# One add of two output-projection weights moved from VectorE to an accumulating transfer, with all jobs in a new order

## The chip, the cores and the metric

The kernel runs on one core of one Trainium2 chip. The metric is the device time of one execution in microseconds (us), lower is better. The core has TensorE (PE), which multiplies matrices; VectorE (DVE) and ScalarE (ACT), which work elementwise; GpSimd (POOL), which here only issues transfers that add to their destination; and SyncE (SP), which issues plain transfers. Each of these takes its own instructions strictly in order, and they meet at semaphores.

## The reference

One layer of a decoder on 512 tokens of width 1024, in f32. Cut to what matters here:

```python
def _mixer(x, mem, ..., w_in, w_a_out, ..., w_b_out, w_kv, w_att_out, w_o):
    h = _rmsnorm(x, norm_mix_g)
    proj = h @ w_in                       # 11264 columns: gated conv, GLU, queries, three gates
    ...                                   # y_a: short conv; y_b: 31-tap conv; y_c: attention on 256 tokens
    g = jax.nn.sigmoid((p_g + b_gate).reshape(bsz, seq, N_BRANCH, D_MODEL))
    merged = g[:, :, 0] * y_a + g[:, :, 1] * y_b + g[:, :, 2] * y_c
    return merged @ w_o                   # w_o: 1024 x 1024

x = x + _mixer(x, ...)
x = x + _conv_ffn(x, ...)                 # up-projection, 3-tap conv, SiLU gate, down-projection
return _rmsnorm(x, norm_final_g)
```

## The kernel before

**Products.** Every f32 operand is split into two float32r parts: ACT casts it to its high part (`whi` for weights, line L1220), and DVE subtracts that from the operand to get the low part (`wlo`, L1224). A product is then three matmuls: high by high, high by low, low by high (L1171 to L1173, and L1424 for the large projections). The large projections, the output projection and the down-projection use a seven-product block scheme (Strassen's): of four weight blocks and four activation blocks, sums and differences are formed, and seven products take the place of eight. A group of such products is a *quad*, its products are numbered 1 to 7, and each needs its own weight sum, split into its own pair `whi`, `wlo`.

**Weight sums.** A block of weights comes from HBM by a plain transfer that SP issues (L1250), 512 KB each. A further block is added in place by a transfer with `accum_op=ALU.add` that POOL issues (L1374, L2479, L2486), which reads its source, adds it to the tile and writes the tile. For one product after the next the same tile goes through several such additions; each waits until the pair of the product before has been split off. There are 48 pairs of transfers for the input projection alone.

**The output projection** (`w_o`, stage "wo", at about 530 to 573 us) has products a, b, f, c, d, e, g, each in two halves i = 0, 1. For half i a tile x holds one weight block plus another (job `("wadd", "x", i)`, a POOL transfer), and a tile y holds a third block. d is split from y, with its low part made by ACT (`("wn", ...)`, a negated copy) and a POOL transfer (`("wl", ("wo", "d", i))`). Then `("wsum", i)` puts y + x into y: by DVE, L1640, 128x1024. c is split from that sum (`("wh", ("wo", "c", i))` on ACT, `("wl", ("wo", "c", i))` on DVE), and after it `("wadd", "y", i)` adds a last block for g.

**Convolution taps.** The 31-tap convolution runs beside the projections: ACT makes products of a tap (`tp`, L2137), pairs of them are joined by a POOL transfer from SBUF to SBUF (`("tj", p, s)`, L2143), and DVE adds them to an accumulator (L2149).

**Attention** takes its scores (job `("s", h, tp)`, L1171 to L1173 on `k` and `qh`, `ql`) from the scaled queries: ACT makes `qh` (L1940), DVE `ql` (L1944).

**The order.** Nothing is scheduled at run time. The table `PLAN` lists all 2457 jobs in the order in which their instructions are emitted, so each engine's queue is the table's subsequence for that engine. An entry holds the job's key, the buffer places that it takes (`wf3` is load buffer 3, `sb7` a slot on the right of SBUF, `ps0` a PSUM bank), and, for some transfers, a third item: the job whose last instruction the transfer must wait for, a *hold*, with which loads are paced. Where a job takes a place, it waits for all users of the tile that held the place before. `Jobs.run` goes through the table and checks that each job stands behind what it needs:

```python
        for key, given, *held in PLAN:
            engine, fn, after, take, use = self.jobs[key]
            ...
            fn()
            if len(code) > n_code:
                for other in held:
                    wait_for(self.tc, code[n_code], last[other])
```

There are 362 jobs on PE, 863 on DVE, 790 on ACT, 185 on POOL and 221 on SP.

Of the kernel before, what the change touches and what calls it, by code (L numbers as in the profile page):

```python
# [11 lines left out]
ALU = mybir.AluOpType  # L12
# [69 lines left out]
    (("mem tile", 0), "sb2"), (("ldm", 0, 0), ""), (("raw tile", "K"), "wf3"),  # L82
# [958 lines left out]
def hybrid_block_kernel(  # L1041
# [19 lines left out]
    nc = tc.nc  # L1061
    x, out = x[0], out[0]
# [2186 lines left out]
```

## Time and profile before

| | us |
|---|---|
| median of 3 runs | 890.8 |
| lowest and highest of them | 887.27, 891.45 |
| the profiled execution | 888.78 |
| its span on the core | 886.8 |
| PE busy | 878.7 |
| DVE busy | 827.2 |
| ACT busy | 701.4 |

The span is the time from the core's first to its last instruction; the profiled execution's own time is 2.0 us longer, for what lies around the span. The page gives the busy time of each engine, the chain of work that ended last, and the groups of instructions; the trace behind it answers for single stretches. On PE matmuls overlap: a row of a matmul shows its whole passage, and the next one starts before it ends, so the distance from start to start is what a matmul costs. PE's granted clock is full in all of the 40 slices of the page.

### The profile page before, as it was taken

What the parts mean: (1) busy time and instruction counts of PE and PEld (TensorE: products, weight loads), DVE (VectorE), ACT (ScalarE), POOL (GpSimd) and SP (SyncE); (2) the same over time, 40 slices, a digit from 0 to 9 for tenths busy, and PEclk for the clock granted to TensorE, in tenths of its full rate; (3) what the DMA queues carried; (4) which work ended last, traced back from release to release, by engine and by line L of the source; (5) the groups of instructions that cost most, each with busy time, mean ns of one, the idle gap of its engine ahead of it and who ended that gap; (6) DMA issues with size and microseconds to landing.
All of it is one profiled execution on the core that took longest, in us unless ns stands there. A gap on an engine that the chain in (4) does not pass through costs nothing.

```text
span 886.8 us, 17492 instructions
## 1 busy us (share of the span) xinstructions
PE 878.7 (99%) x6937; PEld 848.8 (96%) x6937; DVE 827.2 (93%) x949; ACT 701.4 (79%) x983; POOL 168.3 (19%) x193
## 2 busy tenths in 40 slices
PE   9999999999999999999999999999999999999997
PEld 8999999999999999999899998899999999998886
DVE  6997889989999999999899999998899799999997
ACT  7587889979998788798889973877776677866665
POOL 0012222111222131221221211121121111101120
PEclk9999999999999999999999999999999999999999
DMA  9989999779999999998999999999999799689984
GB/s 352 340 194 234 228 254 233 143 148 211 248 232 265 235 266 218 240 245 223 245 228 257 238 251 283 300 261 244 240 236 260 177 262 190 160 284 331 268 180 131
DMA packets 62288, 211.38 MB, mean 238 GB/s; under 512 B 6784, under 2 KB 11776, under 8 KB 62208
## 3 DMA queue, kind: packets, MB, share of 16 engines
q0 software_dynamic: 28944, 96.00, 59.1%
q1 hardware_dynamic: 32976, 114.02, 35.6%
q8 instruction: 54, 0.88, 0.4%
q10 hardware_dynamic: 288, 0.27, 0.1%
q14 instruction: 26, 0.21, 0.1%
HBM read 194.23 MB, written 4.19 MB: 224 GB/s over the span
## 4 chain that ended last, share of the span: by engine, by line
PE 85%; DVE 6%; DMA 3%; ACT 3%; issue 2%; SPq 0%; POOL 0%; DVEq 0%; ACTq 0%
PE bank L1424 61%; PE bank L1173 6%; PE bank L1171 6%; PE bank L1172 6%; PE bank L1810 2%; DVE wlo L1224 2%; PE bank L2331 1%; PE bank L2333 1%; PE bank L2332 1%; DMA wf<-in_w_in 1%; DMA tp<-tp 1%; ACT whi L1220 1%; DVE fl L1338 1%; DMA wf<-in_w_v 1%; ACT tp L2137 1%
## 5 line engine op out<-in xcount | busy, mean ns | idle before, releaser
L1224 DVE TENSOR_TENSOR wlo<-wf,whi 128x1024 fp32r<-128x1024 f32 (+1 forms) x189 | 226.0, 1209 | 13.5 <-ACT whi L1220 13.1
L1220 ACT CAST whi<-wf 128x1024 fp32r<-128x1024 f32 x192 | 198.1, 1042 | 42.6 <-PE bank L1424 13.0
L2137 ACT ACTIVATE tp<-u,pk 128x495 f32<-128x495 f32 (+22 forms) x184 | 119.2, 712 | 4.7 <-DVE acc L2149 1.9
L2149 DVE TENSOR_TENSOR acc<-acc,tp 128x966 f32<-128x966 f32 (+17 forms) x74 | 87.7, 1185 | 4.0 <-DMA tp<-tp 2.1
L1374 POOL DMA_DIRECT2D wf<-in_w_in x48 | 45.9, 990 | 137.1 <-DVE wlo L1224 63.3
L1424 PE MATMUL bank<-fb10h,whi 128*128 128x256 f32 x232 | 64.1, 276 | 0.3 <-ACT bank L1458 0.3
L1424 PE MATMUL bank<-ft4h,whi 128*128 128x256 f32 x232 | 64.0, 276 | 0.0
L1424 PE MATMUL bank<-fb11h,wlo 128*128 128x256 f32 x232 | 63.9, 275 | 0.0
L1424 PE MATMUL bank<-ft7h,whi 128*128 128x256 f32 x232 | 63.9, 275 | 0.0
L1424 PE MATMUL bank<-fb11h,whi 128*128 128x256 f32 x232 | 63.9, 275 | 0.0
L1424 PE MATMUL bank<-fb00h,whi 128*128 128x256 f32 x232 | 63.9, 275 | 0.0
L1424 PE MATMUL bank<-fb00l,whi 128*128 128x256 f32 x232 | 63.8, 275 | 0.0
L1424 PE MATMUL bank<-fb00h,wlo 128*128 128x256 f32 x232 | 63.8, 275 | 0.0
L1424 PE MATMUL bank<-fb10l,whi 128*128 128x256 f32 x232 | 63.8, 275 | 0.0
L1424 PE MATMUL bank<-fb10h,wlo 128*128 128x256 f32 x232 | 63.8, 275 | 0.0
L1424 PE MATMUL bank<-ft5l,whi 128*128 128x256 f32 x232 | 63.8, 275 | 0.0
L1424 PE MATMUL bank<-ft5h,wlo 128*128 128x256 f32 x232 | 63.8, 275 | 0.0
L1424 PE MATMUL bank<-ft6l,whi 128*128 128x256 f32 x232 | 63.8, 275 | 0.0
L1424 PE MATMUL bank<-ft6h,wlo 128*128 128x256 f32 x232 | 63.8, 275 | 0.0
L1424 PE MATMUL bank<-ft7l,whi 128*128 128x256 f32 x232 | 63.8, 275 | 0.0
L1424 PE MATMUL bank<-ft7h,wlo 128*128 128x256 f32 x232 | 63.8, 275 | 0.0
L1424 PE MATMUL bank<-ft4l,whi 128*128 128x256 f32 x232 | 63.8, 275 | 0.0
(434 smaller groups left out, 3371.3 us busy)
## 6 DMA issues: line engine op xcount, KB each, us to landing
wf<-in_w_in POOLq DMA_DIRECT2D x48, 512.0 KB, 7.9
wf<-in_w_in SPq DMA_DIRECT2D x45, 512.0 KB, 6.4
wf<-in_w_up SPq DMA_DIRECT2D x29, 512.0 KB, 6.2
wf<-in_w_up POOLq DMA_DIRECT2D x26, 512.0 KB, 8.2
wf<-in_w_down SPq DMA_DIRECT2D x15, 512.0 KB, 5.3
wf<-in_w_a_out SPq DMA_DIRECT2D x8, 512.0 KB, 5.6
wf<-in_w_v SPq DMA_DIRECT2D x7, 512.0 KB, 6.1
wf<-in_w_kv SPq DMA_DIRECT2D x7, 512.0 KB, 6.8
```

Source lines behind the costliest of these rows:

```text
L1171: nc.tensor.matmul(ps, s_hi, w_hi, start=start, stop=False, skip_group_check=again)
L1172: nc.tensor.matmul(ps, s_hi, w_lo, start=False, stop=False, skip_group_check=again)
L1173: nc.tensor.matmul(ps, s_lo, w_hi, start=False, stop=stop, skip_group_check=again)
L1220: nc.scalar.copy(parts[0], src())
L1224: nc.vector.tensor_tensor(lo, src(), hi.bitcast(F32), op=ALU.subtract)
L1338: nc.vector.tensor_tensor(t, x, y.bitcast(F32), op=ALU.subtract)
L1374: nc.gpsimd.dma_start(out=tiles[key], in_=block(w, col[c], k), accum_op=ALU.add)
L1424: nc.tensor.matmul(ps[:, c, :], w[:, i, at], in_turns(a[i]), start=first and n == 0, stop=i == 3 and n == 2, skip_group_check=again,)
L1810: nc.tensor.matmul(ps[:, j, :], w[:, k, at], in_turns(a[:, k, :]), start=first and j == 0 and k == 0 and n == 0, stop=g == 1 and k == 3 an ...
L2137: nc.scalar.activation(two(("tp", p, s))[:, j, s:], two(("u", p))[:, j, : SEQ - s], AF.Copy, scale=weight(j),)
L2149: nc.vector.tensor_tensor(a, a, two(("tp", p, at))[:, :, at:], op=ALU.add)
L2331: nc.tensor.matmul(ps, w_hi[:, i, at], hi, start=first, stop=False)
```

## The change

`("wsum", 0)` becomes a POOL transfer that adds tile x to tile y inside SBUF; `("wsum", 1)` stays on DVE. The job needs what it needed before, and c's first half is split from its result as before.

```diff
         deferred.append(lambda i=i: job(
             ("wsum", i), "DVE", dve(1024), lambda: add_into(("wo", "y", i), ("wo", "x", i)),
-            [("wadd", "x", i), ("wl", ("wo", "d", i))], use=[("wo", "x", i), ("wo", "y", i)]))
+            [("wadd", "x", i), ("wl", ("wo", "d", i))], use=[("wo", "x", i), ("wo", "y", i)])
+            if i else job(
+            ("wsum", i), "POOL", MORE, lambda: nc.gpsimd.dma_start(
+                out=tiles["wo", "y", i], in_=tiles["wo", "x", i], accum_op=ALU.add),
+            [("wadd", "x", i), ("wl", ("wo", "d", i))], MORE_LATENCY,
+            use=[("wo", "x", i), ("wo", "y", i)]))
```

The whole table `PLAN` is replaced: the same jobs in another order, with other buffer places and other holds. Of PE's 362 jobs 89 change their rank, by at most 6 places; of DVE's 653, of ACT's 612, of POOL's 99 and of SP's 157, by up to 34. Two of its lines:

```diff
-    (("ld", ("raw", ("K", 0, 1))), "wf0", ("mh", 0, 0)), (("V", 0, 0), ""),
...
+    (("V0",), "ps0 ps2"), (("mh", 0, 1), ""), (("wl0", "V"), ""), (("ldm", 1, 0), "", ("warm",)),
```

What moved is shown at three places. The first is POOL's queue at the output projection (`whol` is a low part that a transfer finishes, `wo` the tiles x and y and that of e). Before:

```order
L1241 DMA whol_824_6423<-in_w_o 128x1024
L2479 DMA wo_847_6612<-in_w_o 128x1024
L1241 DMA whol_861_6718<-in_w_o 128x1024
L2479 DMA wo_855_6678<-in_w_o 128x1024
L1241 DMA whol_879_6855<-in_w_o 128x1024
L2479 DMA wo_876_6847<-in_w_o 128x1024
L2479 DMA wo_884_6878<-in_w_o 128x1024
L2486 DMA wo_854_6649<-in_w_o 128x1024
L2486 DMA wo_869_6807<-in_w_o 128x1024
```

and after:

```order
L1240 DMA whol_810_6315<-in_w_o 128x1024
L2478 DMA wo_820_6392<-in_w_o 128x1024
L2478 DMA wo_852_6648<-in_w_o 128x1024
L1240 DMA whol_862_6720<-in_w_o 128x1024
L2485 DMA wo_856_6681<-wo_820_6392 128x1024
L1240 DMA whol_881_6859<-in_w_o 128x1024
L2478 DMA wo_877_6851<-in_w_o 128x1024
L2478 DMA wo_884_6877<-in_w_o 128x1024
L2490 DMA wo_856_6681<-in_w_o 128x1024
L2490 DMA wo_870_6806<-in_w_o 128x1024
```

The new transfer (L2485) stands behind the one that finishes d's low part, and the addition into x's first half has moved up two places; behind the new one stand five more transfers of this stage. On DVE the add is gone there, and on PE the first group of d's matmuls, six of them, now stands ahead of c's first.

The second place is at about 183 to 191 us, ahead of the scores of heads 2 and 3. DVE (`acc<-acc,tp` adds a tap, `ql` is the queries' low part), before:

```order
L1224 TENSOR_TENSOR wlo_315_2332<-wf_266_1956,whi_314_2331 128x1024
L2149 TENSOR_TENSOR acc_290_2143<-acc_290_2143,tp_300_2245 128x2x511
L2149 TENSOR_TENSOR acc_290_2143<-acc_290_2143,tp_307_2303 128x2x509
L1944 SCALAR_TENSOR_TENSOR ql_330_2405<-qq_288_2136,qh_323_2379 128x1024
L1944 SCALAR_TENSOR_TENSOR ql_332_2434<-qq_269_1963,qh_322_2377 128x1024
```

and after:

```order
L1223 TENSOR_TENSOR wlo_316_2353<-wf_280_2063,whi_315_2352 128x1024
L2148 TENSOR_TENSOR acc_295_2172<-acc_295_2172,tp_298_2211 128x2x511
L1943 SCALAR_TENSOR_TENSOR ql_324_2381<-qq_270_1991,qh_318_2359 128x1024
L1943 SCALAR_TENSOR_TENSOR ql_326_2392<-qq_271_1995,qh_323_2379 128x1024
L1223 TENSOR_TENSOR wlo_321_2369<-wf_299_2215,whi_320_2368 128x1024
```

The second tap's add has left the place ahead of the queries, and head 2's queries, which come first on PE, are now first here too (`qh_322` and `qh_318` are head 2's). Two things do not show in these rows. Head 2's `qh` took the place of a tile `tp` that a joining transfer read, and now takes one that attention's softmax has left. And on PE the 24 matmuls of product 5 of the quad `("gate", 2, 1)` stood ahead of these scores, and now stand behind them.

The third place is ACT at about 357 to 362 us (L1458 seeds one PSUM bank with another; `wf_521` before and `wf_557` after are the tile of weight sums of the quad `("bb", 1)`). Before:

```order
L1220 CAST whi_600_4661<-wf_583_4518 128x1024
L1220 CAST whi_602_4665<-('cv', 3)_524_3994 128x1024
L1220 CAST whi_604_4694<-wf_521_3988 128x1024
L1458 COPY bank_606_4698<-bank_599_4635 128x512
L2137 ACTIVATE tp_607_4701<-u_185_1225,pk_86 128x489 x2
```

and after:

```order
L1219 CAST whi_599_4659<-wf_527_4002 128x1024
L2136 ACTIVATE tp_601_4664<-u_178_1159,pk_86 128x489 x2
L1219 CAST whi_602_4669<-('bb', 1)_583_4494 128x1024
L1457 COPY bank_604_4696<-bank_598_4633 128x512
L1465 ACTIVATE B_606_4701<-bank_591_4564 128x2x256
L1219 CAST whi_607_4703<-wf_557_4280 128x1024
```

The copy of the bank stood behind the cast of the quad's weight sum, and now stands ahead of it.

## Rows read from the trace of the kernel before

**Rows 1.** Page, part 1: busy us, share of the span, instructions.

```profile
PE 878.7 (99%) x6937; PEld 848.8 (96%) x6937; DVE 827.2 (93%) x949; ACT 701.4 (79%) x983; POOL 168.3 (19%) x193
```

**Rows 2.** Chain that ended last: start us, us, what.

```profile
175.71 10.53 DMA tp<-tp
...
348.82 11.48 DMA wf<-in_w_in
...
582.96 190.28 PE bank L1424 x1704
```

**Rows 3.** Page, part 5: line, engine, operation, tiles, count; busy us, mean ns; idle before.

```profile
L1224 DVE TENSOR_TENSOR wlo<-wf,whi 128x1024 fp32r<-128x1024 f32 (+1 forms) x189 | 226.0, 1209 | 13.5 <-ACT whi L1220 13.1
L1220 ACT CAST whi<-wf 128x1024 fp32r<-128x1024 f32 x192 | 198.1, 1042 | 42.6 <-PE bank L1424 13.0
...
L1424 PE MATMUL bank<-ft5h,wlo 128*128 128x256 f32 x232 | 63.8, 275 | 0.0
```

**Rows 4.** Waits of PE: waited for; us in total, times, longest.

```profile
PE bank L1171 <- ACT ob L2032: 0.7, 1, 0.7
PE bank L1424 <- ACT bank L1458: 0.3, 1, 0.3
PE bank L1173 <- DVE ql L1944: 0.2, 1, 0.2
PE bank L1810 <- DVE wlo L1224: 0.2, 1, 0.2
PE bank L1173 <- DVE mgl L2527: 0.2, 1, 0.2
```

**Rows 5.** ACT in order of time, 186 us: start, us, what, idle before.

```profile
186.26 2.01 ACT L1940 ACTIVATE qh<-qq 128x1024 fp32r<-128x1024 f32 x2 [3.14 <-DMA tp<-tp]
```

**Rows 6.** DVE in order of time, at 186 and at 541 us.

```profile
186.26 2.48 DVE L2149 TENSOR_TENSOR acc<-acc,tp 128x1022 f32<-128x1022 f32 x2 [2.11 <-DMA tp<-tp]
188.65 2.35 DVE L1944 SCALAR_TENSOR_TENSOR ql<-qq,qh 128x1024 fp32r<-128x1024 f32 x2
...
540.93 1.21 DVE L1640 TENSOR_TENSOR wo<-wo,wo 128x1024 f32<-128x1024 f32 x1
542.06 1.81 DVE L2527 TENSOR_TENSOR mgl<-mg,mgh 128x512 fp32r<-128x512 f32 x2
```

**Rows 7.** POOL in order of time: the addition into x's first half.

```profile
532.04 0.86 POOL L2479 DMA_DIRECT2D wo<-in_w_o  x1 [1.26 <-PE bank L1424]
```

**Rows 8.** Line L2143, the joins inside SBUF: 18 transfers of about 500 KB.

```profile
DMA to landing us min/median/max: 4.9/7.0/10.5
```

**Rows 9.** Tile wo, 520 to 565 us: its transfers from HBM.

```profile
DMA to landing us min/median/max: 5.2/6.9/11.1
```

**Rows 10.** PE in order of time, at 550, 714 and 736 us.

```profile
550.24 0.38 PE L1171 MATMUL bank<-whi,mgh 128*128 128x512 f32 x1
550.46 0.38 PE L1172 MATMUL bank<-wlo,mgh 128*128 128x512 f32 x1
...
714.23 0.28 PE L1424 MATMUL bank<-ft6l,whi 128*128 128x256 f32 x1
...
735.78 0.28 PE L1424 MATMUL bank<-ft5h,wlo 128*128 128x256 f32 x1
```

**Rows 11.** Page, part 3: queue of POOL's transfers; packets, MB, share of 16 engines.

```profile
q0 software_dynamic: 28944, 96.00, 59.1%
```

**Rows 12.** Busy time by stretch: us, engines, clock, DMA share, GB/s.

```profile
480.00:545.00 65.00, 64.83 (x499) 61.93 (x498) 62.98 (x83) 53.14 (x71) 12.30 (x15) 1.00 1.02 260
545.00:600.00 55.00, 54.94 (x381) 51.13 (x380) 52.83 (x61) 40.48 (x56) 11.04 (x13) 1.00 1.03 269
```

**Rows 13.** Line L1250, the plain loads of weights that SP issues.

```profile
DMA to landing us min/median/max: 3.6/6.3/12.1
```

**Rows 14.** Line L1374, the additions into weight tiles that POOL issues.

```profile
DMA to landing us min/median/max: 5.5/8.0/12.5
```

More of the change, by code (lines that the diff above doesn't have):

```diff
@@ L534 @@
-    (("wl", (("gate", 1, 0), 7)), ""), (("tap", 3, 30), ""), ((("gate", 1, 1), 5), "ps6"),
-    (("wh", (("gate", 1, 1), 1)), ""), (("weigh", 0, 2, 1), ""),
[4 rows of a table removed]
-    (("mu", "low"), ""), (("weigh", 0, 2, 0), ""),
-    (("ld", ("raw", ("merge", 0, 3, 0))), "wf3", ("tap", 3, 27)), (("mu", "mean"), "ps0"),
-    (("wh", (("gate", 1, 0), 3)), ""), (("r7", ("gate", 1, 0)), ""), ((("gate", 1, 1), 1), "ps1"),
-    (("centre", 1), ""), (("wh", (("gate", 1, 1), 2)), ""), (("sum", 0, 2), "", ("mu", "mean")),
@@ L614 @@
-    (("sum", 1, 1, 0), ""), ((("out", 1, 1), 3), ""), (("r3", ("out", 1, 0)), ""),
-    (("mgh", "a", 1), ""), (("wl", ("wo", "a", 1)), ""), (("mgh", "b", 0), "sb3"),
-    (("wl", ("wo", "d", 0)), "", (("out", 1, 0), 3)), (("by3", ("out", 1, 0)), ""),
-    ((("out", 1, 1), 4), ""), (("mgl", "a", 1), ""), (("r3", ("out", 1, 1)), ""),
-    (("sum", 1, 0, 1), "sb12"), (("wadd", "x", 0), "", (("out", 1, 1), 3)),
[105 rows of a table removed]
-    ((("cf", 1, 1), "done"), ""), ((("cf", 1, 0), "done"), ""), (("silu", 1), ""),
[18 rows of a table removed]
-    ((("cf", 2, 1), "done"), ""), ((("cf", 2, 0), "done"), ""), (("silu", 2), ""),
[34 rows of a table removed]
@@ new lines @@
+    (("o", 3, 0), "ps6"), (("ptl", 2, 1), ""), (("wl", (("cv", 0), 1)), ""),
+    (("wh", (("gate", 2, 1), 7)), ""), (("s3", ("gate", 2, 1)), ""), ((("gate", 2, 1), 6), ""),
[26 rows of a table added]
+    (("wl", (("out", 2, 0), 2)), ""), (("tap", 1, 16), ""), ((("out", 2, 1), 1), "ps7"),
[4 rows of a table added]
+    (("wl", (("out", 2, 1), 5)), ""), (("wh", (("out", 2, 1), 2)), ""), (("tap", 1, 18), ""),
+    ((("out", 2, 0), 5), "ps1"), (("r1", ("out", 2, 1)), "ps4"), (("s6", ("out", 2, 1)), ""),
+    (("wl", (("out", 2, 1), 2)), ""), (("sigmoid", 2, 3), ""), (("by2", ("out", 2, 0)), ""),
@@ new lines @@
+    (("fl", "o2", "t6"), ""), ((("out", 2, 1), 2), ""), (("wh", (("out", 2, 0), 7)), ""),
+    (("s7", ("out", 2, 1)), "", (("out", 2, 1), 1)),
+    (("ld", (("out", 2, 0), "r")), "wf2", ("fl", "o2", "t6")), (("tp", 1, 21), "sb15"),
+    (("wl", (("out", 2, 0), 7)), ""), (("wh", (("out", 2, 0), 6)), ""), (("tap", 1, 19), ""),
[8 rows of a table added]
+    (("wh", (("out", 2, 0), 4)), ""), (("tap", 1, 22), ""),
[119 rows of a table added]
+    (("wh", (("gate", 0, 0), 2)), ""), (("tap", 2, 24), ""),
[21 rows of a table added]
+    (("tap", 2, 29), ""), (("s6", ("gate", 0, 1)), "", (("gate", 0, 1), 5)),
@@ new lines @@
+    ((("gate", 0, 1), 1), "ps2"), (("wh", (("gate", 0, 0), 3)), ""), (("tap", 3, 3), ""),
+    (("tp", 2, 30), "sb15"), (("r7", ("gate", 0, 0)), ""), (("tap", 3, 4), ""),
+    (("s7", ("gate", 0, 1)), "", ("wh", (("gate", 0, 1), 2))), ((("gate", 0, 0), 4), ""),
[3 rows of a table added]
+    (("tap", 2, 30), ""), (("wh", (("gate", 1, 0), 5)), ""),
+    (("ld", ("raw", ("merge", 0, 0, 0))), "wf0"), (("tp", 3, 7), "sb3"),
+    (("wl", (("gate", 0, 1), 6)), ""), ((("gate", 0, 0), 3), ""),
[6 rows of a table added]
+    (("r6", ("gate", 0, 1)), ""), (("wh", (("gate", 1, 0), 1)), ""), (("tap", 3, 8), ""),
@@ new lines @@
+    (("wh", ("merge", 0, 0, 1)), ""), (("tap", 3, 13), ""),
+    (("ld", ("raw", ("merge", 0, 2, 0))), "wf0", ("wl", ("merge", 0, 0, 0))), (("tap", 3, 14), ""),
+    (("tp", 3, 15), "sb7"), (("merge", 0, 0, 0), "ps2 ps0"), (("tp", 3, 18), "sb2"),
+    (("tap", 3, 15), ""), (("wl", ("merge", 0, 0, 1)), ""), (("tp", 3, 17), "sb7"),
+    (("tap", 3, 16), ""), (("ld", ("raw", ("merge", 0, 2, 1))), "wf3", (("gate", 1, 0), 2)),
+    (("wh", ("merge", 0, 1, 1)), ""), (("tj", 3, 18), "", ("tp", 3, 13)),
@@ new lines @@
+    (("wn", ("merge", 0, 1, 1)), ""), (("merge", 0, 0, 1), ""), (("sigmoid", 0, 1), ""),
+    (("wh", ("merge", 0, 1, 0)), ""), (("wl", ("merge", 0, 1, 1)), "", ("tp", 3, 18)),
+    (("sigmoid", 0, 0), ""), (("wl", ("merge", 0, 1, 0)), ""), (("wh", ("merge", 0, 2, 0)), ""),
[4 rows of a table added]
+    (("wl", ("merge", 0, 2, 0)), "", ("sigmoid", 0, 0)), (("tap", 3, 19), ""),
+    (("tp", 3, 21), "sb7"), (("wh", ("merge", 0, 2, 1)), ""), (("tap", 3, 20), ""),
+    (("tp", 3, 22), "sb2"), (("sum", 0, 0), ""), (("merge", 0, 1, 1), ""), (("tap", 3, 21), ""),
@@ new lines @@
+    (("wh", (("gate", 1, 0), 6)), ""), (("tap", 3, 22), ""), (("tp", 3, 23), "sb7"),
+    (("wl", (("gate", 1, 0), 6)), ""), (("s5", ("gate", 1, 1)), "", ("merge", 0, 1, 0)),
+    (("wn", ("merge", 0, 2, 1)), ""), (("tap", 3, 23), ""), (("tap", 3, 24), ""),
+    (("tp", 3, 25), "sb7"), ((("gate", 1, 0), 6), ""),
+    (("wl", ("merge", 0, 2, 1)), "", ("tp", 3, 22)), (("r2", ("gate", 1, 0)), "sb2"),
+    (("weigh", 0, 1, 1), ""), (("tap", 3, 25), ""), (("weigh", 0, 1, 0), ""),
+    (("ld", (("gate", 1, 1), "u")), "wf0", (("gate", 1, 0), 6)), (("merge", 0, 2, 0), "ps4 ps0"),
@@ new lines @@
+    (("tp", 3, 26), "sb7"), ("tot1", "lf0"), (("wh", (("gate", 1, 0), 4)), ""), (("sum", 0, 1), ""),
+    (("tap", 3, 26), ""), (("r6", ("gate", 1, 0)), ""), (("wl", (("gate", 1, 0), 4)), ""),
+    (("tp", 3, 27), "sb7"), (("wh", (("gate", 1, 1), 5)), ""), ("tot2", "", ("merge", 0, 1, 1)),
+    (("tap", 3, 27), ""), (("merge", 0, 2, 1), ""), (("wl", (("gate", 1, 1), 5)), ""),
+    (("wh", (("gate", 1, 0), 7)), ""), (("sigmoid", 0, 2), ""), (("tap", 3, 28), ""),
[3 rows of a table added]
+    (("tap", 3, 30), ""), ((("gate", 1, 0), 7), ""), (("wh", (("gate", 1, 1), 1)), ""),
@@ new lines @@
+    ((("gate", 1, 0), 3), ""), (("wh", (("gate", 1, 1), 7)), ""), (("var", "sum"), ""),
[5 rows of a table added]
+    (("wh", ("merge", 0, 3, 1)), ""), (("wl", (("gate", 1, 1), 4)), ""), (("sigmoid", 1, 0), ""),
[6 rows of a table added]
+    (("table", "swish"), ""), (("s5", ("out", 1, 0)), "", ("r5", ("gate", 1, 1))), (("lns", 2), ""),
+    (("wh", (("gate", 1, 1), 3)), ""), (("lns", 1), ""), (("swish", 0), ""),
+    (("merge", 0, 3, 1), ""), (("wl", (("gate", 1, 1), 3)), ""),
[4 rows of a table added]
+    ((("gate", 1, 1), 4), ""), (("s7", ("out", 1, 0)), "", ("wh", (("gate", 1, 1), 3))),
@@ new lines @@
+    (("fl", "o1", "b00"), ""), (("wh", (("out", 1, 1), 1)), ""), (("swish", 3), ""),
+    (("weigh", 0, 3, 0), ""), ((("out", 1, 0), 1), "ps1"), (("weigh", 0, 3, 1), ""),
[12 rows of a table added]
+    ((("out", 1, 0), 2), ""), (("table", "last"), ""), (("r3", ("gate", 1, 1)), ""),
+    (("o1", "t4"), ""), (("wh", (("out", 1, 0), 7)), ""), (("wl", (("out", 1, 1), 2)), ""),
+    ((("out", 1, 1), 5), "ps2"), (("sigmoid", 1, 2), ""),
+    (("sum", 0, 3), "", ("r3", ("gate", 1, 1))), (("by2", ("out", 1, 0)), ""),
[4 rows of a table added]
+    (("s3", ("out", 1, 0)), "", (("out", 1, 1), 5)), (("sum", 1, 0, 0), "sb1"),
@@ L964 @@
+    ((("out", 1, 0), 6), ""), (("wh", (("out", 1, 1), 6)), ""), (("wl", (("out", 1, 0), 4)), ""),
[15 rows of a table added]
+    ((("out", 1, 1), 3), ""), (("wadd", "x", 1), "", ("wl", (("out", 1, 1), 4))),
[6 rows of a table added]
+    (("sum", 1, 1, 1), ""), (("by4", ("out", 1, 1)), ""), (("ldr", 0), "sb0"),
[264 rows of a table added]
+    (("silu", 10, 0), ""), ((("cf", 10, 0), 0, "half", 1), ""),
[77 rows of a table added]
     ("ends", ""), (("rt", 3), ""), (("rc", 3), ""), (("sa", 3), ""), (("sv", 3, 0), ""),
```

147 lines of the change are left out of this document (42 added, 105 removed), and 1537 rows, old and new, of the table PLAN.

## Prediction

> **What bounds the kernel now.** I read the page's first part, then the chain that ended last, then PE's waits, because the first two say that only the third can change. PE is busy 878.7 us of a span of 886.8, DVE 827.2 [rows 1]. The chain runs for long stretches through PE alone: 1704 matmuls from 583 us on take 190.28 us, 111.7 ns each [rows 2]. A matmul's own row shows 275 ns [rows 3], so a row is 163 ns longer than its place in the queue, and a wait that the profile shows in front of a matmul costs PE about 0.16 us more than the number shown. Behind the wait for its first operands at the start, which both kernels have, PE has five waits of 0.7, 0.3, 0.2, 0.2 and 0.2 us [rows 4]: 1.6 + 5 x 0.16 = 2.4 us. That is all that an order can give back, since the matmuls, their number and their clock stay. The profiled execution took 888.8 us, 2.0 us more than its span, so without a single wait it would have taken **886.4 us**. The median of the three runs, 890.8, is 2.0 us above the profiled one and the lowest is 1.5 below it. As the same program ran, a typical run holds some 4.4 us of such waits; the order's job is to make them rare.
>
> Faster or slower by over 0.5%, about what a measurement of this kernel can tell from no change, is below 886.35 or above 895.25 us against that median. The first is the floor itself.
>
> **The change part by part.** *The add leaves DVE.* One 128x1024 instruction of 1.21 us goes [rows 6]. Right behind it stood the two low parts of the merged activations at 542.06, and PE waited 0.2 us, so 0.36, for the first of them, `mgl` [rows 4, 6]. With the add gone that low part can start up to 1.21 us earlier. What is late next there is its cast on ACT, and 0.36 us is the most that PE gets back, since it waits no longer than that: **-0.36**, bounds 0 and -0.36.
>
> *The add comes to POOL.* Its issue of about 0.9 us [rows 7] lies on an engine that is 19% busy [rows 1]; I cost it at nothing, and 0.9 us on the five transfers behind it is the price if they were late already. What matters is when the sum lands. It waits for the addition into x's first half, issued at 532.04 before [rows 7] and now two places further up, and for d's low part, which keeps its chain of load, cast, negation and transfer. Additions of this stage land 5.2 to 11.1 us after their issue, half of them within 6.9 [rows 9], so 532.0 + 6.9 = 539 is when the new transfer can start, give or take. The nearest rows for its own length are the joins inside SBUF of the same size: 4.9, 7.0 in the middle, 10.5 at the longest [rows 8]. It lands at 546 (544 to 549.5). Behind it come a cast of 1.04 and a difference of 1.21 us [rows 3], with some 0.2 us of handing over. PE wants the low part with the second matmul of c, at 550.46 before [rows 10]; the six matmuls of d that stand ahead of it now make it 1.3 us later, 551.75. So the sum may land as late as 551.75 - 2.45 = 549.3. Spare time in the middle case 3.3 us, at the longest -0.2. **0**, bounds 0 and +0.2; if the transfers that it waits for were also at their longest (11.1), 4.4.
>
> *The attention scores.* At 186.26 both ACT (3.14 us idle) and DVE (2.11 us idle) come out of a wait for the same join inside SBUF, which took 10.53 us [rows 2, 5, 6]. ACT waited because head 2's `qh` took the place of a tile that the join read; DVE because the tap's add stands ahead. Then two tap adds (2.48) and two `ql` (2.35) follow, and PE waits 0.7 and 0.2 us [rows 4, 6]. In the new order `qh` takes a place that the softmax left long before, one of the two tap adds is behind `ql`, and head 2's `ql` is the first of the two. That is 1.2 us for the add and 1.2 for the other head's `ql`, 2.4 us earlier on DVE. PE gives some of it away: the product of 24 matmuls that covered the wait is now behind the scores, 24 x 0.112 = 2.7 us. Against the clock that is no gain at all unless the join lands sooner. It can: its hold on PE's transposes is replaced by one on ACT's tap product. With a join of 7.0 us [rows 8], not 10.5, neither engine waits for it. The two waits are 0.9 + 0.32 = 1.22 us; I take **-1.2**, bounds 0 (the join again at its longest) and -1.22.
>
> *The bank copy.* A weight sum's addition took 11.48 us, the cast that waited for it stood ahead of the bank copy on ACT, and PE waited 0.3 us for the copy [rows 2, 4]. Now the copy is ahead of the cast: **-0.46**. A late landing here holds only its own product, 12 matmuls or more later.
>
> *The start.* PE waited 0.2 us for the low part of one key block [rows 4]. That difference has moved ahead of the second low part of the memory tokens, which PE needs some matmuls later: **-0.36**, bounds 0 and -0.36. Its load is now held back by a cast instead of an earlier one, so I do not count on it fully.
>
> *All other jobs.* The old order's five waits go for at most 0.36 + 1.2 + 0.46 + 0.36 = 2.4 us, to 886.4. But every engine's queue has changed, and the time that a transfer takes is a draw: 3.6 to 12.1 us for a load [rows 13], 5.5 to 12.5 for an addition [rows 14]. New waits are bounded below by nothing and above, in the middle of the cases, by the 4.4 us that the old order's median run holds. I take 1.8, somewhat under half of that, because the places that cost most before are rearranged so that a late landing holds one product and not a queue. **886.4 + 1.8 = 888.2 us.**
>
> **A page against the rows.** By PE's rows the floor is 886.4, because the distance from matmul to matmul leaves nothing between them. The Trainium skill, "Perfetto Trace Analysis", section "Identifying the Most-Contended Engine", says that the busy share of matmuls is a poor measure of headroom and that the share of weight loads should be read instead. Weight loads are busy 848.8 of 886.8 us [rows 1]; read as headroom that would be 38 us, and a better order could end near 849. The trace speaks against it here: 1704 matmuls follow each other at one even distance with no wait in between [rows 2], which no order can shorten. I give it 1 in 100.
>
> **The rivals.** *Clean order.* All five waits go and nothing takes their place: 886.4. For it: each has a named cause that the new order removes. Against it: no run of before is below 887.27. 14 in 100, and about 10 of these are below 886.35.
>
> *No better.* The waits are elsewhere, but as many, since landings set them: 890.8, from 887.3 to 891.5. The freed 1.21 us on DVE is then simply idle time. This is also the case in which the change does nothing that it says: DVE is 61.93 of 65 us busy in the stretch before 545 [rows 12], and one instruction less of 83 moves no wait. 19 in 100.
>
> *The new transfer crowds others.* POOL's transfers hold the 16 DMA engines for 59.1% of the span [rows 11], 0.591 x 886.8 / 185 = 2.8 us for each of the 185. From 480 to 600 us the DMA share is 1.02 and 1.03 [rows 12], so there is no free time for one more: the transfers behind it in the stage's chain land up to 2.8 us later, and with a sum that lands 0.2 late PE waits up to 3 us: 888.2 + 3 = 891.2. By "DMA: Bandwidth & Descriptors", section "Issuing engines are not separate DMA queues", of the Trainium skill, transfers of all issuing engines share the 16 DMA engines and interleave, so SP's loads would wait as well as POOL's; the shares here agree. Against it: the stretch behind has a longer spare time, as PE's waits name no transfer there [rows 4]. 6 in 100.
>
> *Loads held too late: slower.* In the new order the weights of the up-projection's last quads are held behind PE's products. The clearest place is quad 9's tile for product 5: its load was issued at 672 us, over 40 us ahead of its addition, and is now held by the last matmul of quad 7's product 2, which starts about 714.3 [rows 10]. POOL then waits for that load before it issues the addition, with the additions of quad 8 queued behind it. PE wants the low part at 735.78 [rows 10]. In the middle: 714.4 + 6.3, then a second hold to about 721, + 8.0 + 1.04 + 1.21 + 0.2 = 731.5, 4.3 us to spare. At the longest of both: 714.4 + 12.1 + 12.5 + 2.45 = 741.5, a stall of 5.7 us. It decides from where the two landings together take over 18.9 us; the middle is 14.3. One such pair: 888.2 + 5.7 = 893.9. Two in a run, or quad 8's additions too: 899.6. Against it: the two longest of some 200 transfers would have to meet. 8 in 100, nearly all of it above 895.25, since one pair alone is rare enough to sit in the forecast's range.
>
> **How the numbers follow.** Forecast 888.2 with 52 in 100 (886.4 to 890), clean 14, no better 19, crowded 6, held too late 8, the page's headroom 1. The range reaches down to 886.2, which leaves out some 6 (half of the clean case and the page's), and up to 892.0, which takes in "no better" and "crowded" and leaves out the late loads and a few more: 886.2 to 892.0 holds 8 in 10 or somewhat more. Faster by over 0.5%: 10 of the clean case + 1 + 1 of the forecast's own lower end = 0.12. Slower by over 0.5%: 0.07, nearly all late loads. Within: 0.81.
>
> **What would show it.** Right: PE's waits no longer name `ql` or the ACT copy `ob` [rows 4], nor the bank copy, nor `mgl`; their sum is below 2.4 us; the new transfer, line L2485, lands before 549.3 and the cast of c's sum is not waited for by PE; busy time of PE is unchanged, DVE's is 1.2 us less. The step on the attention is wrong if PE waits there for the join as before; that on the transfer if ACT is idle until it lands and PE behind ACT; that on the crowd if loads between 540 and 560 land 2 to 3 us later than now. The prediction as a whole is wrong if PE shows a single wait of over 2 us, or if its waits are as few as forecast and the time differs all the same, since then something outside of PE's queue sets the end.

## The result, and the profile after

The changed kernel takes 890.39 us (median of 22 runs, 888.56 to 897.28), the kernel before 888.87 us (median of 22 runs, 886.57 to 891.45): a ratio of 1.0025, 95% interval 1.0013 to 1.0037. It is slower, by 1.5 us between the medians and 2.2 by the ratio. That lies within 0.5% and inside the range, but it is on the other side of no change than the forecast. The 890.8 us that the prediction set out from was the median of three runs; 22 runs put the kernel before 1.9 us lower. One of the six executions of experiment 2 below took 1128.73 us at a mean granted clock of 0.752 and is left out of its figures.

The profiled execution of the changed kernel took 890.03 us, 2.1 us more than its span. First its page, part 1, in the form of [rows 1]; then PE's waits, in the form of [rows 4].

```profile
PE 878.6 (99%) x6937; PEld 848.9 (96%) x6937; DVE 825.7 (93%) x948; ACT 701.7 (79%) x983; POOL 169.0 (19%) x194
```

```profile
PE bank L1423 <- ACT gt L1453: 2.0, 1, 2.0
PE bank L2738 <- DVE ones L2741: 1.1, 1, 1.1
PE bank L1170 <- DVE x L3068: 0.5, 1, 0.5
```

PE has as much work as before and DVE 1.5 us less. The 1.1 us behind `ones` are the wait at the start that both kernels have. Of the five waits in [rows 4] not one is left. In their place stand two others, and the larger, 2.0 us, is longer than any wait of before. The chain that ended last says what is behind it (start us, us, what):

```profile
588.60 2.28 DVE wlo L1223 x2
590.91 0.47 issue
591.39 9.73 DMA wf<-in_w_up
601.38 0.77 issue
...
603.27 11.05 PE bank L1423 x96
```

A transfer of 9.73 us, issued at 591.39, sets when PE goes on. It is POOL's addition of the weights for quad 1, product 6 of the up-projection. SP's queue, POOL and ACT in order of time at that place (start, us, what, idle before):

```profile
591.00 0.69 SPq L1249 DMA_DIRECT2D ('up', 3)_981_7518<-in_w_up  x1
```

```profile
591.39 1.75 POOL L1373 DMA_DIRECT2D wf<-in_w_up  x2 [2.55 <-DVE wlo L1223]
```

```profile
601.20 1.04 ACT L1219 CAST whi<-wf 128x1024 fp32r<-128x1024 f32 x1 [4.13 <-DMA wf<-in_w_up]
602.15 0.59 ACT L1465 ACTIVATE uu<-bank 128x512 f32<-128x512 f32 x1
602.64 0.58 ACT L1453 COPY gt<-bank 128x512 f32<-128x512 f32 x1
```

ACT is idle for 4.13 us until the addition lands, casts the sum and copies two banks, of which PE waits for the second. But the wait is not only ACT's order: behind the cast VectorE makes the low part until 603.5, and PE needs that with the product's third matmul. What is late is the addition. And 0.4 us ahead of it SP issues a load that the old order sent out at 602.4: quad 3's tile for product 5, called `('up', 3)` here. In the new order it has no hold any more. The same load and the same addition in the trace of before, and that addition's time to land:

```profile
602.38 0.37 SPq L1250 DMA_DIRECT2D ('up', 3)_989_7559<-in_w_up  x1
```

```profile
594.58 0.86 POOL L1374 DMA_DIRECT2D wf<-in_w_up  x1 [1.65 <-DVE wlo L1224]
```

```profile
DMA to landing us min/median/max: 7.1/7.1/7.1
```

The second wait is in the last product, where PE waits for a bank that VectorE has to read; DVE and PE in order of time:

```profile
868.18 0.68 DVE L3068 TENSOR_TENSOR x<-x,bank 128x512 f32<-128x512 f32 x1
```

```profile
868.92 0.48 PE L1170 MATMUL bank<-whi,zh 128*128 128x512 f32 x1 [0.51 <-DVE x L3068]
```

POOL's additions for that stage go out later and closer together than before: the first into tile `y_sum` at 845.9 us where it was 837.3, five more up to 862.5 us. They also take longer. Tile `y_sum` from 838 to 872 us, from issue to landing, the changed kernel first, then the one before:

```profile
DMA to landing us min/median/max: 7.3/9.4/10.4
```

```profile
DMA to landing us min/median/max: 5.7/7.9/8.7
```

### The profile page after: what moved, and what is told of

The parts are those of the page before. It is cut to its first block, busy times and chain, and to the rows that moved or that the text cites. A ratio compares the mean times of both kernels' runs of the same rounds, so it can differ in the third digit from the quotient of the medians.

```text
span 887.9 us, 17483 instructions
## 1 busy us (share of the span) xinstructions
PE 878.6 (99%) x6937; PEld 848.9 (96%) x6937; DVE 825.7 (93%) x948; ACT 701.7 (79%) x983; POOL 169.0 (19%) x194
## 4 chain that ended last, share of the span: by engine, by line
PE 92%; DMA 4%; DVE 2%; issue 1%; ACT 1%; SPq 0%; POOL 0%; DVEq 0%; POOLq 0%; ACTq 0%
PE bank L1423 68%; PE bank L1170 5%; PE bank L1171 5%; PE bank L1172 5%; DMA wf<-in_w_down 2%; PE bank L2330 2%; PE bank L2332 2%; PE bank L2331 2%; PE bank L1809 2%; DMA wf<-in_w_up 1%; DVE wlo L1223 1%; DMA wf<-in_w_kv 1%; PE bank L2612 0%; PE bank L2064 0%; DVE zl L2922 0%
## 5 line engine op out<-in xcount | busy, mean ns | idle before, releaser
L1223 DVE TENSOR_TENSOR wlo<-wf,whi 128x1024 fp32r<-128x1024 f32 (+1 forms) x193 | 230.7, 1210 | 18.6 <-ACT whi L1219 18.4
L1219 ACT CAST whi<-wf 128x1024 fp32r<-128x1024 f32 x196 | 201.9, 1042 | 48.7 <-PE bank L1423 16.2
L2136 ACT ACTIVATE tp<-u,pk 128x494 f32<-128x494 f32 (+22 forms) x184 | 118.9, 709 | 5.8 <-DVE acc L2148 4.8
L2148 DVE TENSOR_TENSOR acc<-acc,tp 128x1022 f32<-128x1022 f32 (+17 forms) x74 | 87.5, 1186 | 1.7 <-ACT tp L2136 0.2
L1373 POOL DMA_DIRECT2D wf<-in_w_in x56 | 51.5, 978 | 185.6 <-PE bank L1423 63.3
L1423 PE MATMUL bank<-ft6h,whi 128*128 128x256 f32 x232 | 63.9, 275 | 2.0 <-ACT gt L1453 2.0
L1423 PE MATMUL bank<-ft4h,whi 128*128 128x256 f32 x232 | 64.0, 276 | 0.1
L1423 PE MATMUL bank<-fb10h,whi 128*128 128x256 f32 x232 | 64.0, 276 | 0.0
L1423 PE MATMUL bank<-fb00h,whi 128*128 128x256 f32 x232 | 64.0, 276 | 0.0
L1423 PE MATMUL bank<-fb11h,whi 128*128 128x256 f32 x232 | 63.9, 275 | 0.0
L1423 PE MATMUL bank<-ft7h,whi 128*128 128x256 f32 x232 | 63.9, 275 | 0.0
L1423 PE MATMUL bank<-ft6h,wlo 128*128 128x256 f32 x232 | 63.9, 275 | 0.0
L1423 PE MATMUL bank<-fb00h,wlo 128*128 128x256 f32 x232 | 63.8, 275 | 0.0
L1423 PE MATMUL bank<-fb10l,whi 128*128 128x256 f32 x232 | 63.8, 275 | 0.0
L1423 PE MATMUL bank<-fb10h,wlo 128*128 128x256 f32 x232 | 63.8, 275 | 0.0
L1423 PE MATMUL bank<-ft5h,whi 128*128 128x256 f32 x232 | 63.8, 275 | 0.0
L1423 PE MATMUL bank<-ft5l,whi 128*128 128x256 f32 x232 | 63.8, 275 | 0.0
L1423 PE MATMUL bank<-ft5h,wlo 128*128 128x256 f32 x232 | 63.8, 275 | 0.0
L1423 PE MATMUL bank<-ft6l,whi 128*128 128x256 f32 x232 | 63.8, 275 | 0.0
L1423 PE MATMUL bank<-ft7l,whi 128*128 128x256 f32 x232 | 63.8, 275 | 0.0
L1423 PE MATMUL bank<-ft7h,wlo 128*128 128x256 f32 x232 | 63.8, 275 | 0.0
L1423 PE MATMUL bank<-ft4l,whi 128*128 128x256 f32 x232 | 63.8, 275 | 0.0
```

The lines of the kernel that those rows point to most:

```text
L1219: nc.scalar.copy(parts[0], src())
L1223: nc.vector.tensor_tensor(lo, src(), hi.bitcast(F32), op=ALU.subtract)
L1373: nc.gpsimd.dma_start(out=tiles[key], in_=block(w, col[c], k), accum_op=ALU.add)
L1423: nc.tensor.matmul(ps[:, c, :], w[:, i, at], in_turns(a[i]), start=first and n == 0, stop=i == 3 and n == 2, skip_group_check=again,)
L2136: nc.scalar.activation(two(("tp", p, s))[:, j, s:], two(("u", p))[:, j, : SEQ - s], AF.Copy, scale=weight(j),)
L2148: nc.vector.tensor_tensor(a, a, two(("tp", p, at))[:, :, at:], op=ALU.add)
```

## Experiments

All ratios are to the kernel before, run on the same chip. Theory A: the new order behind 583 us costs the time. Rival B: the added transfer crowds the others. Rival C: new waits ahead of 583 us. The table of orders is one list for all engines; a row in the diffs below is a job, its place in memory, and the job that it is held by. Up to 583 us (1624 jobs) and again up to 757 us (2099 jobs) both orders have done the same set of jobs, so that one order can be continued by the other; where a place in memory was still taken behind such a seam, the job got another free one.

**1. The add back on VectorE, in the new order.**

```
 (("wl", ("wo", "f", 0)), ""),
+(("wsum", 0), ""),
...
-            if i else job(
-            ("wsum", i), "POOL", MORE, lambda: nc.gpsimd.dma_start(
-                out=tiles["wo", "y", i], in_=tiles["wo", "x", i], accum_op=ALU.add),
```

> The new order, but the one add is an instruction of VectorE again (1.21 us), put behind the two low parts of f, where VectorE stands at about 541.7 us. Theory A (the new order from 583 us on costs the time: the weights of the up-projection and of the last stage land too late and PE waits, 2.0 us at 603.3 and 0.5 us at 868.9 in the profile of the changed kernel): the add has nothing to do with it, 890.4 us, 1.0017 of before. Rival B (the added transfer crowds the others): back to before, 888.9, 1.000. Rival C (new waits ahead of 583 us, the start among them): 890.4 as well.

Measured: 1.0021 (1.0009 to 1.0034). The loss is as large without the added transfer, as far as the intervals tell, so B falls for the new order. In the changed kernel the five additions that stand behind the new transfer also land after 5.5 to 10.2 us, against 6.0 to 11.1 in the trace of before. PE's longest wait is that of the changed kernel (here L2997 is its L1423):

```profile
PE bank L2997 <- ACT gt L3027: 1.5, 1, 1.5
```

**2. The transfer alone, in the old order.** Only the definition of the job changes.

> The old order, with the one add as POOL's transfer at its old place. Theory A and rival C: the transfer alone costs little; its sum can start at 539 at the earliest, lands at 544 to 549.5, and PE wants what is made of it (2.45 us later) at 550.46, so 888.9 in the middle case and at the longest landing 1.5 us of wait. ACT's cast of the sum stands at 544.4 in the old order and what is queued behind it on ACT waits with it: up to 890. Rival B: 890.4 or more, with the additions behind it landing 2 to 3 us later.

Measured: 1.0051 (1.0036 to 1.0066), 893.92 us. The transfer costs 4.5 us where it stands alone. A and C missed this. B's figure (890.4 or more) and its sign came true, since the two additions behind the new one took 8.9 and 11.4 us where the trace of before has 6.0 and 8.8; but PE waits for the sum itself, not for those. It went out at 539.0, as expected, and landed 9.8 us later, amid four loads of the residual that SP had issued between 534 and 539. ACT's queue in order of time, then PE:

```profile
548.89 1.04 ACT L2793 CAST whi<-wo 128x1024 fp32r<-128x1024 f32 x1 [5.26 <-DMA wo<-wo]
549.84 1.99 ACT L4100 CAST mgh<-mg 128x1024 fp32r<-128x1024 f32 x2
```

```profile
550.93 0.48 PE L2744 MATMUL bank<-whi,mgh 128*128 128x512 f32 x1 [1.71 <-ACT mgh L4100]
...
553.33 0.64 PE L2745 MATMUL bank<-wlo,mgh 128*128 128x512 f32 x1 [1.91 <-DVE wlo L2797]
553.76 0.63 PE L2746 MATMUL bank<-whi,mgl 128*128 128x512 f32 x1
```

Behind the cast that waits for the sum stand two casts of activations, the later of them ready at 545, and DVE stands idle for 5.25 us behind them. PE waits twice, 3.6 us in all. Then its matmuls come 0.43 us apart, not 0.216, from 553.3 to 556.7. The busy times by stretch (the two figures behind POOL's count are the granted clock and the DMA share) show why:

```profile
550.00:553.00 3.00, 0.48 (x1) 0.19 (x1) 2.08 (x2) 1.83 (x2) 0.00 (x0) 1.00 1.05 240
553.00:557.00 4.00, 3.67 (x9) 2.95 (x10) 4.00 (x6) 0.00 (x0) 1.75 (x2) 0.57 0.85 206
```

The mean granted clock from 553 to 557 us is 0.57: most of that stretch is at the lower of its two levels, 1.2 and 2.4 GHz. Eight matmuls at 0.21 us more each are another 1.7 us. So the new order around the output projection is what makes the transfer affordable: there its sum is issued at 531.45 and lands at 540.0, 5 us ahead of its cast.

```profile
531.45 0.86 POOL L2485 DMA_DIRECT2D wo<-wo  x1 [2.75 <-DMA wo<-in_w_o]
```

```profile
DMA to landing us min/median/max: 8.6/8.6/8.6
```

**3 and 4. Half and half: the old order up to 583 us and the new one behind, and the reverse.**

> The old order up to the place where both orders have done the same set of jobs (583 us, all of the output projection and the first of the up-projection behind), the add on VectorE, and from there on the new order. Theory A: 890.4 us, 1.0017 of before, with a wait of PE near 603 us behind ACT in part of the runs. Rivals B and C: 888.9, 1.000.

> The other way round: the new order with the transfer up to 583 us, and the old order from there on. Theory A: 888.9 us or below it, down to 887.3 if the waits of the old order at 190, 362 and 543 us (1.2 + 0.4 + 0.3 us in the profile of before) are gone for good. Rivals B and C: 890.4.

Measured: 1.0021 (1.0008 to 1.0034) with the new order behind 583 us, 0.9995 (0.9981 to 1.0008) with it ahead. A stands, and C falls as the cause of the loss. The trace of the first has the old waits at 190 and 543 us and the new one near 605 side by side:

```profile
PE bank L2997 <- ACT gt L3027: 1.2, 1, 1.2
...
PE bank L2744 <- ACT ob L3605: 0.8, 1, 0.8
...
PE bank L2746 <- DVE ql L3517: 0.2, 1, 0.2
```

The second did not come down to 887.3: its trace has none of the waits of [rows 4], but three on weights between 602 and 627 us, 1.8 us in all, behind the seam, and two of 0.5 and 0.3 us at 544 and 558 us, ahead of it. The first of the three is behind quad 1's addition again, which took 8.2 us. At the other two the trace shows loads that go out early: two of SP, at 617.25 and 617.66 in the trace of before, stand at 608.28 and 608.70 here, beside three additions of POOL issued from 607.92 to 611.23, which took 9.0, 12.3 and 12.0 us and not 7.1, 7.2 and 8.7 (the second of them also stands 0.5 us behind the first now and not 2.4). The later of the two loads, in the trace of before and here, and the first two of these additions here:

```profile
617.66 0.45 SPq L1250 DMA_DIRECT2D ('up', 3)_1006_7758<-in_w_up  x1
```

```profile
608.70 0.39 SPq L2823 DMA_DIRECT2D ('up', 3)_1006_7758<-in_w_up  x1
```

```profile
DMA to landing us min/median/max: 9.0/10.6/12.3
```

The jobs behind the seam got other places in memory at nine points, which may be what lets these loads go earlier; that was not tested.

**5 and 6. The one load: held back in the new order, sent early in the old one.**

```
-(("ld", (("up", 3), "s")), "lf4"),
...
 (("ld", (("up", 1), "r")), "wf0", ("r2", ("up", 0))),
+(("ld", (("up", 3), "s")), "lf4", (("up", 0), 7)),
```

```
+(("ld", (("up", 3), "s")), "lf3"),
 (("ld", (("up", 1), "r")), "wf4", ("wl", (("up", 0), 7))),
...
-(("ld", (("up", 3), "s")), "lf0", (("up", 1), 5)),
```

> The changed kernel with one load moved: SP's load of up-projection quad 3's tile for product 5, which the new order issues at 591.0 us, 0.4 us ahead of POOL's addition for quad 1's product 6, is put behind the next load on SP and held by the end of the fourth product ahead of that one (about 598.6 us). Theory A1 (that load shares the DMA engines with the addition and makes it land 9.2 to 9.7 us after its issue, where the old order had 7.1 and PE can wait for 9.7 at most): the addition lands in 7 to 8 us, PE's wait at 603 us (2.0 us in the changed kernel, 1.5 with the add on VectorE, 1.2 with the old front) is gone, 888.6 us, 0.9997 of before. Rival A2 (the wait there is a matter of the products' order and of chance): it stays, 890.4, 1.0017.

> The other way round in the old order: the same load, which the old order issues at 602.4 us, goes out right behind the load ahead of it on SP, at about 591.1 us, into a tile that is free since 565 us (the load behind it takes the tile that this one had); one cast and one difference that the program wants ahead of it stand one place earlier on ACT and VectorE. Theory A1: the addition of quad 1's product 6 lands 9 to 10 us after its issue at 594.6 and not 7.1, and PE waits there for 0 to 1.5 us: 889.5 to 890.5, 1.001 to 1.002. Rival A2: 888.9, 1.000.

Measured: 0.9994 (0.9983 to 1.0005) with the load held, 1.0014 (1.0002 to 1.0026) with it early in the old order. Both times went as A1 said. With the load held the addition lands in 8.2 us, and PE's wait is 0.6 us; A1 had it gone:

```profile
DMA to landing us min/median/max: 8.2/8.2/8.2
```

```profile
PE bank L2997 <- ACT gt L3027: 0.6, 1, 0.6
```

In the old order four other loads had to take other places as well, and one cast and one difference moved up. The early load went out at 593.73, with this execution 2.6 us late by then, and lay 1.1 us ahead of the addition of quad 0's product 3, not of quad 1's product 6; it was that one that PE waited for. Its landing, 6.9 us in the trace of before, is now:

```profile
DMA to landing us min/median/max: 9.9/9.9/9.9
```

```profile
605.82 0.38 PE L2997 MATMUL bank<-fb11h,whi 128*128 128x256 f32 x1 [1.48 <-ACT whi L2793]
...
607.08 0.38 PE L2997 MATMUL bank<-fb11h,wlo 128*128 128x256 f32 x1 [0.77 <-DVE wlo L2797]
```

This trace is weaker evidence than the times: its execution, 895.84 us, was the longest of the twelve, and an addition issued at 587.70, 6 us ahead of the load, took 9.8 us as well. It shows something else. Behind these two waits the granted clock falls (the two figures behind POOL's count are again the clock and the DMA share), and from 608.2 to 611.4 us matmuls come 0.21 us apart and not 0.11, which costs 1.5 us more:

```profile
608.00:612.00 4.00, 4.00 (x24) 4.00 (x23) 2.59 (x4) 3.60 (x6) 0.86 (x1) 0.57 0.99 283
```

**7 and 8. The old order behind 757 us, without and with the load held.**

> The changed kernel up to the last point at which both orders have done the same jobs (757 us), and the old order behind it. In the new order eight additions of the last product lie between 846 and 863 us, each landing 8 to 10 us after its issue; in the old one half of them go out by 844 us. PE waits at 868.9 us for a bank that VectorE reads late (0.5 us shown, 0.68 lost, and 0.16 at 862.9). If these waits are the new order's own: 0.3 to 0.8 us back, 889.8 us, 1.0010 of before, and no wait of PE behind 840 us. If they are chance: 890.4.

> Both repairs at once in the changed kernel: the load moved as in the first of these, and the old order behind 757 us. Theory A1 with the last stage's waits as the new order's own: 890.4 - 1.8 - 0.6 = 888.0 us, 0.999 of before, and what is left of PE's waits is below 2 us in all. If the new order's waits are spread over many places by chance: 890 or more.

Measured: 1.0008 (0.9996 to 1.0019), and 0.9984 (0.9973 to 0.9996) with both, 887.99 us. In neither trace does PE wait behind 840 us. With the old end alone the wait near 603 is still there, 1.6 us; with both it is 0.3:

```profile
PE bank L2997 <- ACT gt L3027: 1.6, 1, 1.6
```

```profile
PE bank L2997 <- ACT gt L3027: 0.3, 1, 0.3
```

The order with both repairs is faster than the kernel before by 0.16% (0.04 to 0.27), and than the changed one by some 0.4%.

**9 and 10. The addition sent earlier, with both repairs and without any.** The low part for which the addition waits is made one place earlier, and the addition's hold on a product of PE goes.

```
-(("wh", (("up", 0), 7)), ""),
...
 (("wh", (("up", 1), 5)), ""),
+(("wh", (("up", 0), 7)), ""),
...
-(("wl", (("up", 0), 7)), ""),
...
 (("wl", (("up", 1), 5)), ""),
+(("wl", (("up", 0), 7)), ""),
...
-(("s6", ("up", 1)), "", (("up", 2), 2)),
+(("s6", ("up", 1)), ""),
```

> The kernel with both repairs, and in it the addition of quad 1's product 6 goes out earlier: it waits for VectorE's low part of quad 1's product 5 (the same tile), which is now made ahead of that of quad 0's product 7 (one cast and one difference change places), and the addition's hold on a product of PE is taken away. It can go out at about 590.3 us and not 591.4 to 592.8. PE waited there for 0.3 us (0.49 lost) with both repairs. If what counts is the time from the addition's issue to PE's product (9.7 us in the changed kernel, 8 to 8.3 needed with the load held, plus 2.4 for cast and difference): that wait goes, 887.5 us, 0.998 of before. If the landing grows by as much as the issue comes earlier: 888.0, as with both repairs alone.

> The changed kernel with that exchange and without that hold, and nothing else: the load that crowds the addition stays where the new order has it (591 us). The addition goes out 1.1 us earlier, partly ahead of the load. If the 9.1 to 9.7 us that it takes to land stay: PE's wait at 603 us falls from 1.5 to 2.0 us to 0.4 to 0.9, 889.3 us, 1.000 to 1.001 of before. If the issue ahead of the load also shortens the landing to 8: no wait at 603, 888.6, 0.999. If the landing only grows by as much: 890.4.

Measured: 0.9985 (0.9976 to 0.9995) and 0.9984 (0.9971 to 0.9997). The exchange alone, 888.08 us, is worth as much as the other repairs together, and adds nothing to them. In its trace, 1.5 us late by then, the addition goes out at 591.49, now 1.3 us ahead of the load, takes 8.9 us and lands in time, 11.0 us being left to PE's product at 602.52:

```profile
591.49 0.86 POOL L2947 DMA_DIRECT2D wf<-in_w_up  x1 [1.18 <-DVE wlo L2797]
```

```profile
592.82 0.46 SPq L2823 DMA_DIRECT2D ('up', 3)_981_7518<-in_w_up  x1
```

This is all that PE waits for behind the start:

```profile
PE bank L2744 <- DVE x L4160: 0.3, 1, 0.3
```

With all three at once the profiled execution was a long one, 892.09 us, and shows a wait that no earlier trace had:

```profile
PE bank L2997 <- DVE V L3043: 1.7, 1, 1.7
```

It is at 359 us. The wait near 603 us, which was to go, is still 0.5 us there. A load that SP issued at 341 landed after 12.5 us (8.4 in the changed kernel's trace), the cast that waited for it held ACT's queue, and VectorE and PE waited in turn.

**11 and 12. The exchange with the old end, and the exchange with the add on VectorE.**

> The changed kernel with the exchange at the first products of the up-projection (the low part of quad 1's product 5 ahead of that of quad 0's product 7, the addition behind it not held), and the old order behind 757 us. The exchange alone gave 888.1 us (0.9984 of before), the old end alone 0.5 us to 1.0 us against the changed kernel. If the last stage's waits are still in some executions of the exchange alone: 887.5 us, 0.998 of before. If they were gone with it already (its profile had none): 888.1.

> The changed kernel with the exchange, and the one add an instruction of VectorE again (1.21 us at about 541.7 us). It tells what the added transfer is worth once the wait at 603 us is out of the way. If it is worth nothing, as between the changed kernel and the one with the add on VectorE: 888.1 us, 0.9985 of before. If the 1.21 us that VectorE saves reach PE: 888.5 to 889.3. If the transfer crowds the others: 887.5.

Measured: 0.9984 (0.9971 to 0.9998), 887.87 us, and 0.9988 (0.9976 to 1.0001), 888.62 us. Once the addition is in time, the old end adds nothing that the runs can tell. The add as a transfer against the add on VectorE is 0.9984 against 0.9988 here, and 1.0025 against 1.0021 without the exchange: no difference, either way. The profiled execution of the first was at 890.6 us and has the wait at 359 us again, behind the same load, 2.2 us long:

```profile
DMA to landing us min/median/max: 12.9/12.9/12.9
```

## Why the prediction was wrong, step by step

**The floor and the accounting held.** In the changed kernel's trace the waits that are not in every execution are 2.0 and 0.5 us plus 0.16 each, 0.3 and 0.2 at 20 and 614 us, and 0.2 at 863 us that only the distance of the matmuls shows: 3.5 us, on the floor of 886.4, against 890.03 measured. The lowest of all runs is 885.78 us (experiment 11), so the floor is good to some 0.6 us. The rule of the Trainium skill, "Perfetto Trace Analysis", section "Identifying the Most-Contended Engine", that TensorE's headroom is read from the busy share of weight loads and from the share of peak arithmetic, does not hold for the weight loads here: with one wait of 0.3 us left behind the start, experiment 10's profiled execution still took 887.84 us.

**The base was mis-sized.** "A typical run holds some 4.4 us of such waits" rested on three runs. With 888.87 for the median it holds 2.5, which is what the profiled execution showed all along. The old order left less to gain than the forecast took for given: against that median the same 888.2 us is a gain of 0.1% and not 0.3%.

**The five waits went, as forecast.** The scores (-1.2), the bank copy (-0.46), the low part of the key block (-0.36) and `mgl` (-0.36): the first three are in none of the ten traces that have the new order ahead of 583 us, and the last one, at 0.3 us, in one of them (experiment 9, behind its long wait at 359 us). In the four traces with the old order there (before, experiments 2, 3 and 6) the wait at the bank copy is in two and each of the others in three. At 190 us the join now landed in 6.3 us, not 10.53, and `qh` and `ql` come well ahead of the scores:

```profile
182.76 1.11 ACT L1939 ACTIVATE qh<-qq 128x1024 fp32r<-128x1024 f32 x1
```

**The added transfer cost nothing, as forecast,** though not by the terms given. The addition into x's first half went out 10 us earlier than in [rows 7], not a little, and so did the sum: landed at 540.0, not at 546. What the prediction did not see is how much of that the new places of its neighbours were worth. The old order with the same transfer loses 4.5 us: a late sum holds ACT's whole queue behind the cast, where the prediction costed PE's wait for its own product alone, and the lower clock came on top.

**The step that failed is "All other jobs".** It allowed 1.8 us for new waits, "because the places that cost most before are rearranged so that a late landing holds one product and not a queue". They came to 3.5 us in the trace and to 4.0 by the median, and the largest did not come at random. There the reason given does not hold: the late landing held the cast and, behind it in ACT's queue, the bank copy that PE waited for. The wait is there in every trace of the unrepaired new order behind 583 us, 1.2 to 2.0 us long (the changed kernel and experiments 1, 3 and 7). From the addition's issue to PE's product were 9.7 us in the old order (594.58 to 604.24) and as many in the new one (591.39 to 603.27 less the 2.16 that were lost); cast and difference need 2.4 of them. A landing of 7.1 fits and one of 9.7 does not.

In the three traces of the new order in which the load goes out 0.4 to 0.6 us ahead of the addition (the changed kernel and experiments 1 and 7) it took 9.1 to 9.7 us, and PE waited 1.5 to 2.0. In the three in which the load is held (experiments 5 and 8, and 9 with the addition earlier) it took 8.0 to 8.7, and PE waited 0.3 to 0.6. So the load makes some 1.2 us of the landing and of the wait. That it does was shown by holding it alone (experiment 5 against the changed kernel, 0.9994 against 1.0025; 8 against 7, 0.9984 against 1.0008). That the wait hangs on what is left from issue to use was shown by sending the addition earlier, with the load beside it (experiment 10). Why the addition takes some 1 us longer in the new order without the load than the 7.1 of before stays open. In experiment 3 the load is not the cause: it went out 2.4 us behind the addition, which took 8.0 us, and PE waited 1.2 us because the addition was issued only 8.8 us ahead.

Smaller waits of the new order are ahead of 583 us: 0.2 to 0.7 us at 544 to 547 us, for the low part of a weight, in five of the ten traces, and 0.3 us at 558 to 562 us, for a bank, in seven. The changed kernel's own trace has neither.

The wait probably has one more price, which the changed kernel's trace does not show. The mean granted clock is 0.997 or less in 13 of the 58 executions of the four kernels with that wait (they took 891.0 to 897.3 us), and in none of the 84 of experiments 4, 5 and 8 to 12, nor in the 108 of the kernel before that were run beside the experiments. Experiments 2 and 6 show in their traces how waits of PE are followed by a stretch at the lower clock. That it is the wait near 603 us which does this in the 13 is likely but not shown, since no trace of one of them was taken. They make the long runs and not the median: the other 18 runs of the changed kernel have one of 890.2.

**The rivals.** "Crowds others" had the right mechanism, a transfer that is added to a full stretch and makes those beside it late, and its price of up to 3 us. It put it to the wrong transfer: to the one that the change adds, and not to a load that the new order lets go 11 us earlier. In the old order it fits the new transfer too: in experiment 2 the two additions behind it landed 2.9 and 2.6 us later than before. By "DMA: Bandwidth & Descriptors", section "Issuing engines are not separate DMA queues", of the Trainium skill, transfers that SP and POOL start run on the same 16 DMA engines and interleave. The 1.2 us by which SP's load lengthens POOL's addition agree with that. "Loads held too late" looked at the right stage with the wrong sign: quad 9's load was issued at 713.8, as worked out, landed after 5.9 us and its addition at 727.5, and nobody waited. What hurt was the load that came too early. The up-projection was searched for holds that the new order adds, and not for those that it takes away.

**The last stage** had been named in no step. Its additions are bunched behind 845 us and cost 0.68 + 0.16 us in the profiled execution; with the old order there they are not in the trace (experiment 7). But of the six traces with the new end only two have the longer one (the changed kernel and experiment 3), and by experiment 11 the old end is worth nothing beyond what the runs scatter.

**What it would have been.** With that one exchange the new order takes 888.1 us, where 888.2 was forecast. That the two agree is luck, as the forecast knew nothing of the exchange. The gain against the kernel before is then 0.16% (0.03 to 0.29); the kernel before took 889.27 us beside it and not 890.8.

**Open.** Why in two of the ten traces of the new front the transfers issued from 339 to 341 us took 1.5 to 4.6 us longer than in the changed kernel's trace. The wait at 359 us that follows may be part of the changed kernel's long runs too. The longest of them, 897.28 us, has the lowest granted clock of the 22, 0.995, which those two executions do not have.

## What to carry to other kernels

A new order is read as much by the waits that it takes away as by those that it adds: where a transfer loses its hold, ask which transfer on the path will then have company, and how many microseconds lie between that one's issue and its use. Where a chain leaves 7.3 us for a landing that takes 7 to 8 alone and 9.1 to 9.7 beside another, issuing it 1 us earlier did as much here as moving the neighbours. A cast that waits for a transfer is costed with everything that stands behind it in its engine's queue.

## What the runs showed of the hardware that was not expected

- One load of 512 KB issued 0.4 to 0.6 us ahead of an addition of 512 KB lengthened its landing by some 1.2 us (9.1 to 9.7 us against 8.0 to 8.7 in the same order without it), and the addition right behind took 11.9 to 12.7 us against 10.2 to 10.3.
- Two waits of PE, one soon behind the other, were followed by 3.4 us at the lower clock level: 1.7 and 1.9 us in experiment 2 (1.7 us more), 1.5 and 0.8 us in experiment 6 (1.5 us more). One wait of 2.0 us (the changed kernel at 603 us) was not: the 96 matmuls behind it took 11.05 us, 0.115 each.
- A join inside SBUF that adds, like the new transfer, landed in 8.2 to 9.8 us in this stretch, where the 18 joins of before had 7.0 in the middle.
